# A pair's third key chunk and second half of its queries behind its second query group, the output weights and the half projection one group later

## The chip, the cores and the metric

The kernel runs on one core of a Trainium2 chip. The metric is the device time of one execution in microseconds (us). An execution was also taken by the hardware profiler, which gives each instruction's start and length on the core's engines: TensorE (PE for its matmuls, PEld for its weight loads), VectorE (DVE), ScalarE (ACT), GpSimd (POOL) and SyncE (SP), which here only issues transfers.

## The reference

One layer of a trunk over 1024 frames and 16 meta tokens in front, 1024 channels wide, all in float32. What the change touches is the attention group (8 heads of 64) and the output projection behind it:

```python
u = rms_norm(h, norm_mix_w[l])
proj = u @ w_in[l]
fq, fk, fv, ff, hq, hf, hi, hg = jnp.split(proj, split_at, axis=-1)
...
s = jnp.einsum('bqhd,bkhd->bhqk', q_i, k) * scale
s = s + (c_i[..., :, None] - cT[:, :, None, :])      # c: running sum of the log forget gates
s = jnp.where(key_pos[None, :] <= q_pos[:, None], s, MASK_VALUE)
p = jax.nn.softmax(s, axis=-1)
o = jnp.einsum('bhqk,bkhd->bqhd', p, v)
...
mixed = jnp.concatenate([fox_out, hgrn_out], axis=-1) @ w_out[l]
h = h + mixed
```

`hgrn_out` is a second group, a gated linear recurrence, whose four blocks of 128 channels are finished before the attention starts. After this come a norm, a SwiGLU feed-forward part and a final norm.

## The kernel before, in words

Each float32 operand of a large product is split into a rounded part ("hi") and the rest ("lo"), and a product is three matmuls: hi by hi, hi by lo, lo by hi (`mm3`, lines 166 to 169). ScalarE writes "hi" (a cast), VectorE subtracts to get "lo".

The normed input, transposed and split, stays in on-chip memory as `u` (the pool `uT`). The heads go in four pairs, p = 0 to 3. For a pair, `fox_proj` loads its key and query weights (128 columns each) and makes the keys in three chunks of 348, 346 and 346 frames (`keys(0)` to `keys(2)`) and the queries in two halves of 512 (`queries(0)`, `queries(1)`). Each is 24 matmuls into one "dense" accumulator bank, of which there are three, and is then copied out by ScalarE and VectorE (lines 522, 523 and 530, 531).

`fox_compute` then takes the pair's queries in four groups of 256, g = 0 to 3. A group takes for each of its two heads two tiles of 128 queries: scores (lines 569 and 570, tile `g`, two banks), minimum with the bias on VectorE (line 575), exponential on ScalarE (line 580), transposes (lines 588 and 600), copies split in two parts (lines 604 and 605), and the product with the values (line 610). Before it, GpSimd makes a copy of the queries with the two halves swapped (`QB`, lines 555 and 556) and masks (`dm`, line 563). Because the attention is causal, group 0 needs only the first key chunk, group 1 the second too, and groups 2 and 3 all three. Groups 0 and 1 use the first half of the queries, groups 2 and 3 the second.

`fox_proj` makes `keys(0)` and `queries(0)` at once and hands the remaining three back as `rest`, which `fox_compute` calls after group 0. The next pair's `fox_proj` follows group 3 in the code. The key and query weights of a pair lie in two buffers that the next pair's weights take when they are free; their "lo" part is made by GpSimd (line 136).

The last pair calls `after_group(g)` behind each group. After group 0 it gives up the memory of `u`, opens in its place the pools for the output projection, and loads the output weights of the recurrence's blocks (`WO1`, four tiles of 128 x 1024, through two staging buffers, lines 678 to 684). After group 1 it computes `out_half`: the recurrence's part of the output projection for the first two tiles of frames (48 matmuls), and loads the other four weight tiles (`WO2`). Behind the attention follow `out_proj` for the eight tiles of frames, the norm and the feed-forward part.

The order of the code is not the order on the engines. The library with which the program is built orders each engine's instructions by its own estimate of when their operands are ready, and takes the order of the code between those that are. So projections of a pair stand between the matmuls of the group that precedes them in the code, and a transfer is issued when a buffer comes free. On the chip each engine runs its list in order.

Of the kernel before, what the change touches and what calls it, by code (L numbers as in the profile page):

```python
# [44 lines left out]
def f32(ap):  # L45
    return ap.bitcast(F32)
# [3 lines left out]
def hybrid_trunk(  # L50
# [71 lines left out]
    def bank(tag, bufs=None):  # L122
        return (psg if tag in ("g", "o") else ps).tile([P, 512], F32, name=tag, tag=tag, **({"bufs": bufs} if bufs else {}))
# [30 lines left out]
    def load_m(c0, wsrc, engine=None):  # L154
        st = w1.tile([P, KT, P], F32, name="w_st", tag="w_st")
        sync.dma_start(out=st, in_=wsrc.rearrange("(k p) c -> p k c", p=P)[:, :, c0:c0 + P])
        hi = w1.tile([P, KT, P], F32R, name="w_hi", tag="w_hi")
        lo = w1.tile([P, KT, P], F32R, name="w_lo", tag="w_lo")
        split(hi, lo, st, engine)
        return hi, lo  # L160
# [10 lines left out]
    def form1(u, w, c0, n):  # L171
        o = dense()
        hi, lo = w
        for k in range(KT):
            mm3(o[:, :n], hi[:, k, :], lo[:, k, :], u[0][:, k, c0:c0 + n], u[1][:, k, c0:c0 + n], k == 0, k == KT - 1)
        return o[:, :n]
# [205 lines left out]
    def keys(out, R, lev):  # L382
        R6 = R.rearrange("p (k r t) -> p r k t", k=2, r=2)
        Z = (out if lev == 1 else out[:, :256])
        for r in range(2):
            if lev == 1:
                Zr = Z.rearrange("p (k r t) -> p r k t", k=2, r=2)[:, r]
                src = R6[:, r]
            else:
                Zr = Z.rearrange("p (k t) -> p k t", k=2)  # L390
                src = R6[:, r].rearrange("p k (a s b) -> p k a s b", s=2, b=lev)[:, :, :, 0, :]
            if r:
                Zr = Zr[:, :, ::-1]
            if lev > 1:
                Zr = Zr.rearrange("p k (a s b) -> p k a s b", s=2, b=lev)[:, :, :, 0, :]
            act.activation(Zr, src, AF.Exp, scale=-1.0)
# [115 lines left out]
    def fox_proj(p, fxk):  # L512
        KS = [fxk.tile([P, L], F32R, name=f"KS{j}", tag=f"KS{j}") for j in range(2)]
        QA = [fxk.tile([P, SEQ], F32R, name=f"QA{j}", tag=f"QA{j}") for j in range(2)]
        wk, wq = (load_m(c + p * P, w_in[0], pool if p else None) for c in (C_FK, C_FQ))
        lanes = [(0, slice(0, 64), slice(64, 128)), (1, slice(64, 128), slice(0, 64))]

        def keys(i):
            c0, n = FULL[i]
            o = form1(u, wk, c0, n)  # L520
            for j, a, b in lanes:
                act.copy(KS[j][a, c0:c0 + n], o[a])
                vec.tensor_sub(KS[j][b, c0:c0 + n], o[a], f32(KS[j][a, c0:c0 + n]))

        def queries(i):
            c0, n = REAL[i]
            o = form1(u, wq, c0, n)
            q = slice(c0 - META, c0 - META + n)
            for j, a, b in lanes:
                act.activation(QA[j][a, q], o[a], AF.Copy, scale=-0.125)  # L530
                vec.scalar_tensor_tensor(QA[j][b, q], o[a], -0.125, f32(QA[j][a, q]), ALU.mult, ALU.subtract)

        keys(0)
        queries(0)
        return KS, QA, lambda: (keys(1), keys(2), queries(1))

    def fox_head_load(p, j, pool_):
        h = 2 * p + j
        vt = pool_.tile([P, NT + 1, P], F32R, name=f"v{j}", tag=f"v{j}", bufs=1)
        sync.dma_start(out=f32(vt[:, :NT, :]), in_=v_dram[:NT, :, h, :].rearrange("t p c -> p t c"))  # L540
        pool.memset(f32(vt[:, NT, :]), 0.0)
        for r0 in (0, 32):
            sync.dma_start(out=f32(vt[r0:r0 + META, NT, :]), in_=v_dram[NT, :META, h, :])
        nl = pool_.tile([P, L], F32, name=f"nl{j}", tag=f"nl{j}", bufs=1 if p == 0 else 2)
        sync.dma_start(out=nl, in_=nl_dram[h, :].partition_broadcast(P))
        tg = small.tile([P, 4], F32, name=f"tg{j}", tag=f"tg{j}", bufs=2)
        vec.tensor_scalar(tg[:, 0:4], nl[:, META + 255::256], -1.0, None, ALU.mult)
        return vt, nl, tg
# [78 lines left out]
    def fox_compute(p, KS, QA, rest, heads=None, extra=None):  # L627
        heads = heads or [fox_head_load(p, j, fx) for j in range(2)]
        for g in range(4):
            mixp = fx.tile([P, 256], F32, name="mixp", tag="mixp")  # L630
            rr = small.tile([P, 2, 2], F32, name="rr", tag="rr")
            for j in range(2):
                fox_group(p, j, g, KS[j], QA[j], *heads[j], rr, mixp)
            rw = fx.tile([P, 2, P], F32, name="rw", tag="rw", bufs=1)
            pool.tensor_copy(rw.rearrange("p i (j d) -> p (i j) d", d=HD), rr.rearrange("p i j -> p (i j)").unsqueeze(2).to_broadcast([P, 4, HD]))
            rb = bank("tr")
            for ii in range(2):
                pe.transpose(rb[:, ii * P:(ii + 1) * P], rw[:, ii, :], ident)
            vec.tensor_mul(mixp, mixp, rb[:, :256])
            sync.dma_start(out=mix_dram[p, :, 256 * g:256 * (g + 1)], in_=mixp)  # L640
            if g == 0:
                rest()
            if extra:
                extra(g)
    a = hgrn_proj(0)
# [13 lines left out]
    fx0 = fx0_pool.__enter__()  # L659
    heads0 = [fox_head_load(0, j, fx0) for j in range(2)]  # L660
    b = fox_proj(0, fxk0)
    hg_pool.__exit__(None, None, None)
    fx_pool, fxk1_pool = right("fx", 2), right("fxk1")
# [4 lines left out]
    for s in range(3):  # L668
        fox_compute(s, *b, heads0 if s == 0 else None)
        if s == 0:  # L670
            fx0_pool.__exit__(None, None, None)
        b = fox_proj(s + 1, (fxk0, fxk1)[(s + 1) % 2])
# [3 lines left out]
    def load_wo(ks):  # L676
        for k in ks:
            st = w1.tile([P, D], F32, name="w_st", tag="w_st")
            sync.dma_start(out=st, in_=w_out[0, k * P:(k + 1) * P, :])
            hi = wo.tile([P, D], F32R, name=f"woh{k}")  # L680
            lo = wo.tile([P, D], F32R, name=f"wol{k}")
            act.copy(hi, st)
            for hs in (slice(0, 512), slice(512, 1024)):
                vec.tensor_sub(lo[:, hs], st[:, hs], f32(hi[:, hs]))
            wos[k] = (hi, lo)
# [4 lines left out]
    def out_half(ts):  # L690
        mt, mh, ml = (op.tile([P, KT, P], d, name=n_, tag=n_, bufs=1) for n_, d in (("mt", F32), ("mh", F32R), ("ml", F32R)))
        for i, t in enumerate(ts):
            a = slice(4 * i, 4 * i + 4)
            sync.dma_start(out=mt[:, a, :], in_=mix_dram[4:8, :, t * P:(t + 1) * P].rearrange("k p c -> p k c"))
            split(mh[:, a, :], ml[:, a, :], mt[:, a, :])
        for i, t in enumerate(ts):
            halves[t] = op.tile([P, D], F32, name="h2", tag="h2")
            for hs in (slice(0, 512), slice(512, 1024)):
                o = dense()
                for k in range(4):  # L700
                    j = 4 * i + k
                    mm3(o, mh[:, j, :], ml[:, j, :], wos[4 + k][0][:, hs], wos[4 + k][1][:, hs], k == 0, k == 3)
                act.copy(halves[t][:, hs], o)

    def after_group(g):
        nonlocal op, wo
        if g == 0:
            uT_pool.__exit__(None, None, None)
            op, wo = op_pool.__enter__(), wo_pool.__enter__()
            load_wo(WO1)  # L710
        if g == 1:
            out_half(ORDER[:2])
            load_wo(WO2)

    fox_compute(3, *b, None, after_group)
    fxk1_pool.__exit__(None, None, None)
    fx_pool.__exit__(None, None, None)
# [477 lines left out]
```

## Time and profile before

| | |
|---|---|
| time of three runs | median 1305.54 us (1304.8 to 1307.61) |
| profiled execution | 1305.52 us, span 1303.8 us |
| TensorE busy | 1270.7 us, 97% of the span |
| VectorE busy | 909.3 us, 70% |
| ScalarE busy | 621.2 us, 48% |
| GpSimd busy | 125.9 us, 10% |
| mean granted TensorE clock | 0.995 |

The span runs from the first instruction's start to the last one's end. A matmul's row shows about 0.39 us for 512 columns although the next starts 0.23 us later, because matmuls overlap; the distance of starts is what one costs. The time in brackets behind a row is the engine's idle time before it, and behind the arrow stands what ended it. A row of a transfer on SyncE is its issue; it lands microseconds later.

### The profile page before, as it was taken

To read this page: it belongs to the slowest core of one execution; us is meant where nothing else is said; L and a number is where in the kernel's file an instruction comes from. 1 tells how busy PE (TensorE), PEld (TensorE's weight loads), DVE (VectorE), ACT (ScalarE), POOL (GpSimd) and SP (SyncE) were. 2 spreads that over 40 slices of the span, in tenths; PEclk is the share of its full clock that TensorE was granted. 3 is DMA by queue.
4 is the path that set the end of the run, shared out by engine and by line. 5 is a ranking of instruction groups with operands and counts; after the bars stand their busy time and mean duration, and the time that the engine had idled before them with its cause. 6 is when DMAs were issued, how large, how long until landed. Compare 5 with 4: busy or idle time off the path is not lost.

```text
span 1303.8 us, 18528 instructions
## 1 busy us (share of the span) xinstructions
PE 1270.7 (97%) x6553; PEld 1065.4 (82%) x6553; DVE 909.3 (70%) x1889; ACT 621.2 (48%) x1334; POOL 125.9 (10%) x257
## 2 busy tenths in 40 slices
PE   7999999999999999899999999999999999999997
PEld 6888898988888888688868888888888888888886
DVE  6448657574687877796798766666666654697777
ACT  6347656464666665664453333233323323433364
POOL 1131101010334342210000000000000000000000
PEclk8999999999999999999999999999999999999999
DMA  7232212123321211633314323333332336954442
GB/s 253 73 98 58 74 44 73 58 58 118 92 79 45 69 52 47 187 100 119 125 49 138 125 83 115 121 111 103 118 121 74 113 121 248 317 188 151 121 169 82
DMA packets 135197, 146.38 MB, mean 112 GB/s; under 512 B 6984, under 2 KB 95368, under 8 KB 135104
## 3 DMA queue, kind: packets, MB, share of 16 engines
q1 hardware_dynamic: 135104, 145.19, 34.6%
q8 instruction: 52, 0.85, 0.3%
q14 instruction: 41, 0.34, 0.1%
HBM read 105.98 MB, written 39.19 MB: 111 GB/s over the span
## 4 chain that ended last, share of the span: by engine, by line
PE 80%; DVE 8%; ACT 5%; DMA 3%; issue 2%; POOL 2%; SPq 0%; POOLq 0%; DVEq 0%; ACTq 0%
PE pb L167 10%; PE pb L169 10%; PE pb L168 10%; PE dense L169 8%; PE dense L167 8%; PE dense L168 8%; PE g L169 4%; PE g L167 4%; PE g L168 4%; PE o L610 2%; PE tr L600 2%; PE g L569 1%; PE g L570 1%; PE g L446 1%; DMA w_st<-in_w_in_dram 1%
## 5 line engine op out<-in xcount | busy, mean ns | idle before, releaser
L167 PE MATMUL dense<-u_hi,w_hi 128*128 128x512 f32 (+2 forms) x384 | 141.7, 369 | 0.0
L169 PE MATMUL dense<-u_hi,w_lo 128*128 128x512 f32 (+2 forms) x384 | 141.3, 368 | 0.0
L168 PE MATMUL dense<-u_lo,w_hi 128*128 128x512 f32 (+2 forms) x384 | 140.9, 367 | 0.0
L168 PE MATMUL pb<-T_lo,bh 128*128 128x512 f32 x352 | 137.2, 390 | 0.2
L169 PE MATMUL pb<-T_hi,bl 128*128 128x512 f32 x352 | 137.1, 390 | 0.1
L167 PE MATMUL pb<-T_hi,bh 128*128 128x512 f32 x352 | 136.9, 390 | 0.2 <-ACT bh L135 0.2
L135 ACT CAST bh<-sS 128x512 fp32r<-128x512 f32 x88 | 54.3, 621 | 144.3 <-PE pb L168 70.3
L135 ACT CAST h_hi<-h_st 128x1024 fp32r<-128x1024 f32 (+1 forms) x43 | 41.8, 971 | 83.7 <-PE o L168 38.2
L168 PEld LDWEIGHTS pb<-T_lo,bh 128*128 128x128 f32 x352 | 66.1, 188 | 15.0 <-DVE T_lo L136 1.1
L169 PEld LDWEIGHTS dense<-u_hi,w_lo 128*128 128x128 f32 x384 | 72.9, 190 | 6.2
L167 PEld LDWEIGHTS pb<-T_hi,bh 128*128 128x128 f32 x352 | 66.1, 188 | 14.6 <-ACT bh L135 0.6
L167 PEld LDWEIGHTS dense<-u_hi,w_hi 128*128 128x128 f32 x384 | 72.6, 189 | 6.5
L168 PEld LDWEIGHTS dense<-u_lo,w_hi 128*128 128x128 f32 x384 | 72.6, 189 | 6.4
L169 PEld LDWEIGHTS pb<-T_hi,bl 128*128 128x128 f32 x352 | 66.1, 188 | 14.2 <-DVE bl L136 0.4
L167 PE MATMUL pb<-w_hi,h_hi 128*128 128x512 f32 x198 | 77.3, 391 | 0.0
L169 PE MATMUL pb<-w_hi,h_lo 128*128 128x512 f32 x198 | 77.2, 390 | 0.0
L168 PE MATMUL pb<-w_lo,h_hi 128*128 128x512 f32 x198 | 77.2, 390 | 0.0
L136 DVE TENSOR_TENSOR w_lo<-w_st,w_hi 128x1024 fp32r<-128x1024 f32 (+1 forms) x41 | 49.6, 1210 | 35.4 <-ACT w_hi L135 35.4
L136 DVE TENSOR_TENSOR h_lo<-h_st,h_hi 128x1024 fp32r<-128x1024 f32 (+1 forms) x43 | 48.3, 1124 | 30.2 <-ACT h_hi L135 29.9
L167 PE MATMUL g<-B_hi,w_hi 128*128 128x512 f32 x168 | 66.6, 396 | 0.9 <-ACT p L865 0.9
L169 PE MATMUL g<-B_hi,w_lo 128*128 128x512 f32 x168 | 66.5, 396 | 0.0
L168 PE MATMUL g<-B_lo,w_hi 128*128 128x512 f32 x168 | 66.3, 395 | 0.0
(861 smaller groups left out, 3328.5 us busy)
## 6 DMA issues: line engine op xcount, KB each, us to landing
w_st<-in_w_in_dram SPq DMA_DIRECT2D x24, 512.0 KB, 4.2
w_st<-in_w_ffn_gate_dram SPq DMA_DIRECT2D x22, 512.0 KB, 3.8
w_st<-in_w_ffn_up_dram SPq DMA_DIRECT2D x22, 512.0 KB, 3.9
B<-in_w_ffn_down_dram SPq DMA_DIRECT2D x20, 512.0 KB, 6.3
h_st<-S SPq DMA_DIRECT2D x20, 512.0 KB, 3.8
h_st<-A SPq DMA_DIRECT2D x15, 512.0 KB, 4.4
A<-g SPq DMA_DIRECT2D x22, 256.0 KB, 2.0
S<-u SPq DMA_DIRECT2D x22, 256.0 KB, 3.0
```

Source lines behind the costliest of these rows:

```text
L135: later(act.copy(hi, src))
L136: return later((engine or vec).tensor_sub(lo, src, f32(hi)))
L167: pe.matmul(o, lhsT=ah, rhs=bh, start=first, stop=False, skip_group_check=skip)
L168: pe.matmul(o, lhsT=ah, rhs=bl, start=False, stop=False, skip_group_check=skip)
L169: pe.matmul(o, lhsT=al, rhs=bh, start=False, stop=last, skip_group_check=skip)
L446: m = pe.matmul(gb[:, k * P:(k + 1) * P], lhsT=X[:, k * P:(k + 1) * P], rhs=X[:, 256 + k * P:256 + (k + 1) * P], start=True, stop=True)
L569: pe.matmul(sc[:, :w], lhsT=QA[:, P * i:P * (i + 1)], rhs=KS[:, c0:c0 + w], start=True, stop=False)
L570: pe.matmul(sc[:, :w], lhsT=QB[:, P * ii:P * (ii + 1)], rhs=KS[:, c0:c0 + w], start=False, stop=True)
L600: pe.transpose(pt[:, o + ii * P:o + (ii + 1) * P], Ss[ii][:, c:c + P], ident)
L610: m = pe.matmul(ob[:, q0:256], lhsT=vt[:, blk, :], rhs=r[:, q0:256], start=blk == NT, stop=blk == 2 * g + 1 and i == 3)
```

## The change

`fox_proj` hands back two functions in place of one: the first makes the second key chunk, the second makes the third key chunk and the second half of the queries. `fox_compute` calls the first after group 0 and the second after group 1. In the last pair, giving up the memory of `u` and loading `WO1` move from behind group 0 to behind group 1, and `out_half` and `WO2` from behind group 1 to behind group 2.

```diff
@@ fox_proj
         keys(0)
         queries(0)
-        return KS, QA, lambda: (keys(1), keys(2), queries(1))
+        return KS, QA, (lambda: keys(1), lambda: (keys(2), queries(1)))
@@ fox_compute
             sync.dma_start(out=mix_dram[p, :, 256 * g:256 * (g + 1)], in_=mixp)
-            if g == 0:
-                rest()
+            if g < 2:
+                rest[g]()
             if extra:
                 extra(g)
@@ after_group
         nonlocal op, wo
-        if g == 0:
+        if g == 1:
             uT_pool.__exit__(None, None, None)
             op, wo = op_pool.__enter__(), wo_pool.__enter__()
             load_wo(WO1)
-        if g == 1:
+        if g == 2:
             out_half(ORDER[:2])
             load_wo(WO2)
```

## Prediction

> **What bounds the kernel now.** I read the page first (engine shares), then a table of busy time by stage over the attention part, then the order of time on TensorE, ScalarE, GpSimd and SyncE in the one stage that stood out. A row of the table gives start:end, length, and busy microseconds of PE, PEld, DVE, ACT and POOL, then the granted clock, the DMA share and GB/s.
>
> ```profile
> span 1303.8 us, 18528 instructions
> PE 1270.7 (97%) x6553; PEld 1065.4 (82%) x6553; DVE 909.3 (70%) x1889; ACT 621.2 (48%) x1334; POOL 125.9 (10%) x257
> 397.00:424.00 27.00, 26.45 (x168) 22.25 (x168) 20.96 (x71) 19.10 (x48) 14.25 (x28) 1.00 0.19 50
> 424.00:447.00 23.00, 22.93 (x156) 19.62 (x155) 21.12 (x73) 15.70 (x31) 6.71 (x18) 1.00 0.19 58
> 447.00:470.00 23.00, 22.84 (x147) 20.30 (x145) 13.71 (x49) 13.41 (x33) 8.98 (x16) 1.00 0.28 83
> 470.00:503.00 33.00, 32.42 (x217) 28.14 (x215) 29.43 (x105) 22.69 (x50) 12.20 (x30) 1.00 0.09 25
> 503.00:524.00 21.00, 20.45 (x130) 18.03 (x129) 11.98 (x36) 9.20 (x26) 5.27 (x16) 1.00 0.22 65
> 524.00:535.00 11.00, 6.50 (x29) 4.34 (x29) 8.22 (x23) 6.12 (x10) 4.64 (x8) 1.00 0.76 237
> 548.00:564.00 16.00, 14.99 (x82) 11.46 (x80) 15.24 (x46) 10.81 (x24) 4.98 (x11) 1.00 0.44 127
> 564.00:585.00 21.00, 20.66 (x136) 17.79 (x137) 19.13 (x59) 13.95 (x32) 1.01 (x3) 1.00 0.26 84
> ```
>
> TensorE is the bound: 97% of the span. The change adds and removes no arithmetic, so it can win only TensorE's idle time in the stages it touches, and can lose only by making more. Pairs 1 and 2 (397 to 503 us) hold 0.55 + 0.07 + 0.16 + 0.58 = 1.4 us of it. The last pair (503 to 585) holds far more: in 524 to 535 TensorE stands still for 11.00 - 6.50 = 4.5 us, with 0.55 before, and 1.01 and 0.34 in its groups 2 and 3. This is the order of time there, TensorE first, the idle time in brackets:
>
> ```profile
> 516.77 0.37 PE L167 MATMUL dense<-u_hi,w_hi 128*128 128x346 f32 x1
> 518.73 0.40 PE L167 MATMUL dense<-u_hi,w_hi 128*128 128x512 f32 x1
> 524.06 0.39 PE L169 MATMUL dense<-u_hi,w_lo 128*128 128x512 f32 x1
> 524.29 0.34 PE L569 MATMUL g<-KS,QA 128*128 128x400 f32 x1
> 524.65 0.29 PE L569 MATMUL g<-KS,QA 128*128 128x264 f32 x1
> 526.56 0.36 PE L569 MATMUL g<-KS,QA 128*128 128x264 f32 x1 [1.50 <-DVE mx L575]
> 528.38 0.28 PE L588 MATMUL tr<-ident,S__6394 128*16 128x128 f32 x1 [1.34 <-ACT S__6394 L580]
> 528.89 0.50 PE L167 MATMUL dense<-woh,mh 128*128 128x512 f32 x1
> 534.80 0.50 PE L167 MATMUL dense<-woh,mh 128*128 128x512 f32 x1 [1.54 <-ACT woh L682]
> 547.50 0.39 PE L169 MATMUL dense<-woh,ml 128*128 128x512 f32 x1
> 547.73 0.31 PE L569 MATMUL g<-KS,QA 128*128 128x328 f32 x1
> 515.22 0.52 DVE L523 TENSOR_TENSOR KS<-dense,KS 64x346 fp32r<-64x346 f32 x1
> 524.49 0.59 ACT L530 ACTIVATE QA<-dense 64x512 fp32r<-64x512 f32 x1 [4.10 <-PE dense L169]
> 524.98 1.98 ACT L682 CAST woh<-w_st 128x1024 fp32r<-128x1024 f32 x2
> 533.70 1.04 ACT L682 CAST woh<-w_st 128x1024 fp32r<-128x1024 f32 x1 [4.34 <-DMA w_st<-in_w_out_dram]
> 543.90 1.04 ACT L682 CAST woh<-w_st 128x1024 fp32r<-128x1024 f32 x1
> 551.34 1.05 ACT L682 CAST woh<-w_st 128x1024 fp32r<-128x1024 f32 x1 [1.37 <-DMA w_st<-in_w_out_dram]
> ```
>
> Group 1's keys are complete at 515.74 (515.22 + 0.52), yet its first score starts only at 524.29: the third key chunk and the second half of the queries (346 and 512 columns), which group 1 does not need, stand ahead of it. Then group 1 runs with nothing beside it. TensorE waits 1.50 us for VectorE's minimum, 1.34 us for the exponential, and 1.54 us for an output-weight cast that waited 4.34 us for its transfer: 4.38 us, nearly all of the hole.
>
> **The change, part by part.** *Third key chunk and second query half behind group 1.* In the last pair what is left of them from 516.6 on is 7.7 us of matmuls (516.6 to 524.3; rows below). The last 24, of 512 columns, go from 518.73 to 524.29, 0.232 us each. Group 1 itself, by tile:
>
> ```profile
> 516.60:524.30 7.70, 7.53 (x36) 6.34 (x36) 1.03 (x2) 0.89 (x2) 1.00 0.06 19
> 524.30:547.70 23.40, 13.96 (x49) 8.29 (x48) 1.38 (x2) 2.82 (x5) 1.00 0.68 214
> 547.70:564.00 16.30, 8.51 (x29) 5.00 (x28) 1.36 (x2) 0.59 (x1) 1.00 0.43 125
> ```
>
> These are the instructions on the projection accumulators alone: 48 weight loads, so 48 matmuls, in group 1's stretch, which are the half projection's: 48 x 0.232 = 11.1 us. Group 1's own TensorE time is then 23.4 - 4.5 - 11.1 = 7.8 us. With the change it starts at about 516.6 beside the 7.7 us of projections and is done at 516.6 + 7.8 + 7.7 = 532.1, its waits filled: **-4.4 us** (1.50 + 1.34 + 1.54). If the projections still run as a block ahead of it, 0.
>
> *Group 2 now stands right behind its projections.* It needs the second query half, so its chain starts only when that half is copied out. From the last projection matmul, 24 x 0.232 us after the first, to the first out-projection matmul that could fill was 528.89 - 524.06 = 4.8 us; the two score chunks for which there are banks fill 2 x 0.36 = 0.7 us of it (524.29 to 524.65 for a chunk), so up to 4.1 us stand open, and the cast's 1.54 us can come again: 5.6 us. The lower end is 0: the planner may drain the query half between group 1's waits, so that group 1's tail covers the copies. Both rows are as near as they get; since the planner ranks the query half behind all of group 1, some of it must be last, but 7.7 us cannot all be, with 4.4 us of holes to fill in group 1. That leaves (7.7 - 4.4) / 7.7 = 43% of the block contiguous, and I take the same share of the wait, 0.43 x 5.6 = **+2.4 us**.
>
> *Output weights and half projection one group later.* Eight transfers, eight casts on ScalarE, sixteen subtractions on VectorE, four splits and 48 matmuls move; none is added. What starts the ladder is the end of the last projection, whose operand's room the weights take: 524.3 before, about 532.1 after, so 7.8 us later by time although one group later by order. Cost on the path: the 5.6 us above and the rival below. The queues it is moved past:
>
> ```profile
> 536.13 11.74 SPq L679 DMA_DIRECT2D w_st<-in_w_out_dram  x4
> 548.40 0.33 SPq L640 DMA_DIRECT2D mix_dram<-mixp  x1
> 461.75 1.05 ACT L135 CAST w_hi<-w_st 128x1024 fp32r<-128x1024 f32 x1 [1.32 <-PE dense L168]
> 462.88 2.40 POOL L136 TENSOR_TENSOR w_lo<-w_st,w_hi 128x1024 fp32r<-128x1024 f32 x1 [7.99 <-ACT w_hi L135]
> ```
>
> On SyncE the last four weight loads wait for free buffers over 11.7 us, and group 1's store of its mix is queued behind them; after, it is group 2's store. Its reader comes only after the pair, so it costs 0; with that cover gone, it would cost about the delay that the queue has, under 12 us, on one tile.
>
> *The other pairs.* The next pair's weights are cast when the key matmuls free a buffer (461.75, behind a projection matmul), so these 1.05 us and GpSimd's 2.40 us move one group later too, ahead of group 2's query copies; in pairs 0 to 2 the next pair's first projections fill behind them. They cost 0 there, and 2.40 us a pair on the path if that cover were gone. Their gain is bounded by the idle time above, 1.4 us in pairs 1 and 2; I take 0, between -1.4 and +1.4, since idle time is already as low ahead of group 1 (447 to 470: 0.16) as within the groups.
>
> **The sum.** -4.4 + 2.4 + 0 = -2.0 us against the profiled execution, 1305.52 us (span 1303.8, 1.7 around it), which stands within 0.02 us of the median of the runs, 1305.54. Forecast: **1303.5 us**, 0.15% less, inside the 0.2% (2.6 us) that a measurement of this kernel can tell from no change. Its own range is 1302.0 to 1305.0.
>
> **Rivals.** *The hole closes for good* (faster): the query half is drained inside group 1, group 2's chain overlaps group 1's tail, and pairs 1 and 2 give some of their 1.4 us. 1305.5 - 4.4 - 0.6 = 1300.5 us. For it: VectorE and ScalarE are at 11.98 and 9.20 of 21 us in 503 to 524 and have room. Against: group 2 needs both copies of the queries before any score.
>
> *The hole moves whole* (the change does not do what it says): all 5.6 us stand in front of group 2, less 4.4 saved: 1306.7. For it: the same ladder of two buffers, the same cast ahead of the same kind of exponential. Pair 0 and 1 may see no move at all, since the planner already ran projections ahead of their group (TensorE idles 0.55 us in 27 in pair 1).
>
> *The weights come too late for group 3* (slower): the half projection is used up in front of group 3, and the output projection that fills group 3 has no weights yet. The last cast came 551.34 - 524.3 = 27.0 us after the ladder's start, so at 559.1 after; the second of those four casts came at +19.6 (543.90), at 551.7 after. Group 2 and the half projection need 16.3 - 1.0 - 28 x 0.232 = 8.8 and 11.1 us from 532.1, so with the 2.4 us group 3 starts at about 554.4. It decides when group 3 starts before 551.7: then it lacks up to 559.1 - 554.4 = 4.7 us of filler. Price: group 2's 2.4 us and these 4.7 less 4.4 saved, 1308.2 us, and more if VectorE, at 15.24 of 16 us in 548 to 564, also has the weights' subtractions there.
>
> *GpSimd held up by VectorE.* The weight subtractions now stand beside group 2's query copies and masks.
>
> ```profile
> 506.34 0.29 POOL L563 TENSOR_SCALAR_AFFINE_SELECT dm<-nl 128x128 f32<-128x128 f32 x1
> 526.48 0.68 POOL L563 TENSOR_SCALAR_AFFINE_SELECT dm<-nl 128x128 f32<-128x128 f32 x1 [14.94 <-DVE mx L575]
> 509.00 0.39 POOL L555 CAST QB<-QA 64x256 fp32r<-64x256 f32 x1 [2.37 <-PE g L570]
> 527.23 0.73 POOL L555 CAST QB<-QA 64x256 fp32r<-64x256 f32 x1
> ```
>
> The mask took 0.29 us alone and 0.68 beside them, a copy 0.39 and 0.73. With one mask and two copies ahead of group 2's second score matmul that is 0.39 + 2 x 0.34 = 1.1 us more on its chain: 1304.6 us. The Trainium skill, SBUF — State Buffer, section "Who interferes with whom", says that a VectorE instruction with two SBUF inputs and a GpSimd instruction that reads SBUF exclude each other for the whole instruction, so it speaks against moving these subtractions to where GpSimd's copies gate the scores. By that rule the loss is as large as a full subtraction each time; the trace agrees in kind, with 0.34 to 0.39 us each.
>
> **How the numbers follow.** Chances: forecast 0.38 (of it 0.10 under 1302.9), hole closes 0.27, hole moves whole 0.12 (0.01 of it above 1308.1), too late for group 3 0.19, GpSimd 0.04. Faster by over 0.2%: 0.10 + 0.27 = 0.37. Slower: 0.01 + 0.19 = 0.20. Within: 0.43. The range goes from the closing case's lower end, 1305.5 - 4.4 - 1.4 less some of the 1.35 us that groups 2 and 3 of the last pair stand idle, 1299.0, to the slower case's price, 1308.5; beyond the ends lies some 0.1 each side.
>
> **What the profile after would show.** Right: the first 400-column score of the last pair at about 517, no TensorE wait over 1 us in group 1, and between the last projection matmul and the first output-projection matmul a hole of 2 to 3 us in front of group 2. Wrong: a hole of 4 us or more there (moved whole), none (closed), or a new wait for an output-weight cast within group 3 (slower). Idle time in pairs 0 to 2 that moves by over 1.5 us would show that my zero for them failed; so would a planner's order that differs outside the attention.

## The result, and the profile after

The changed kernel took 1309.03 us (median of its timing, 1307.09 to 1312.04), the kernel before 1305.64 in the same one: a ratio of 1.0027, 95% interval [1.0019, 1.0035]. It is 0.27% slower, above the forecast of 1303.5 and above the range's upper end of 1308.5. One run of each kernel in that timing was far slower than its others (2577.79 us after, 1359.93 before) and is in neither the ratio nor the range; it was the changed kernel's that was profiled, so the profile shown here is of a second timing (e1). That one gave 1308.27 against 1304.52, 1.0035 [1.0022, 1.0049]; its profiled execution took 1307.18 us, span 1305.5.

The columns of the rows by stage are those of the prediction's table: start:end, length, busy time of PE, PEld, DVE, ACT and POOL, granted clock, DMA share, GB/s. Since both kernels pass a stage at other times, I cut at the same events: the first exponential of pair 0, of pair 1, of pair 2 and of the last pair, the last one's end, and the first feed-forward matmul. Before:

```profile
355.10:397.80 42.70, 40.84 (x274) 35.65 (x274) 36.49 (x138) 27.77 (x66) 17.46 (x47) 1.00 0.28 91
397.80:447.60 49.80, 49.18 (x321) 41.59 (x320) 41.98 (x144) 34.62 (x80) 20.81 (x44) 1.00 0.19 54
447.60:503.10 55.50, 54.76 (x357) 48.09 (x356) 42.76 (x147) 35.56 (x80) 20.73 (x44) 1.00 0.17 49
503.10:576.60 73.50, 67.25 (x394) 55.31 (x391) 57.73 (x166) 44.79 (x96) 17.66 (x40) 1.00 0.42 130
sum 316.40, PE 304.53 PEld 254.98 DVE 248.10 ACT 189.52 POOL 77.09; mean PE 60.91 PEld 51.00 DVE 49.62 ACT 37.90 POOL 15.42
```

After:

```profile
353.70:395.60 41.90, 40.80 (x275) 35.62 (x274) 36.50 (x138) 27.75 (x66) 17.48 (x47) 1.00 0.29 91
395.60:449.30 53.70, 51.62 (x348) 44.99 (x346) 45.20 (x151) 37.11 (x85) 21.71 (x46) 1.00 0.20 61
449.30:506.70 57.40, 55.65 (x346) 48.60 (x346) 41.14 (x145) 33.73 (x77) 21.76 (x47) 0.97 0.12 38
506.70:574.20 67.50, 60.80 (x353) 49.71 (x351) 53.94 (x155) 42.23 (x89) 16.25 (x35) 0.97 0.42 126
sum 319.90, PE 305.88 PEld 257.54 DVE 248.36 ACT 189.53 POOL 77.59; mean PE 61.18 PEld 51.51 DVE 49.67 ACT 37.91 POOL 15.52
```

The sums, which hold the five stretches up to the first feed-forward matmul, differ by 3.5 us, as much as the timings do. Length less PE busy is TensorE's idle time: 11.87 before, 14.02 after, 2.15 us more. The other 1.35 us are in PE's busy time although the work is the same, and the granted clock, 1.00 in every row of before, is 0.97 in two of after.

By stage the idle time is: pairs 1 and 2 together 0.62 + 0.74 = 1.36 before and 2.08 + 1.75 = 3.83 after; the last pair 6.25 and 6.70; pair 0 1.86 and 1.10. So the pairs that the forecast took at zero lost 2.47 us, and the pair that was to win 2.0 won nothing. TensorE's waits for GpSimd's swapped queries (`QB`) from 395 to 505 us, pairs 1 and 2 (what it waited for, us in total, times, the longest), say where. Before, then after:

```profile
PE g L570 <- POOL QB L556: 0.4, 1, 0.4
```

```profile
PE g L570 <- POOL QB L555: 2.6, 2, 1.5
```

The 0.4 us of before stand at 504.69, in the last pair's first group; pairs 1 and 2 had no such wait. The two of after, one a pair, are about as long together as the 2.47 us that these pairs lost. GpSimd's order of time after, in pair 2:

```profile
474.17 2.38 POOL L136 TENSOR_TENSOR w_lo<-w_st,w_hi 128x1024 fp32r<-128x1024 f32 x1 [4.84 <-ACT w_hi L135]
476.61 0.39 POOL L556 CAST QB<-QA 64x256 fp32r<-64x256 f32 x1
477.06 0.74 POOL L555 CAST QB<-QA 64x256 fp32r<-64x256 f32 x2
```

The next pair's weight subtraction, 2.38 us, stands directly ahead of the swapped queries of group 2, and TensorE waits for them:

```profile
475.48 0.57 PE L569 MATMUL g<-KS,QA 128*128 128x328 f32 x2
477.51 0.57 PE L570 MATMUL g<-KS,QB 128*128 128x328 f32 x2 [1.47 <-POOL QB L555]
477.92 0.42 PE L169 MATMUL dense<-u_hi,w_lo 128*128 128x348 f32 x1
...
479.58 0.49 PE L169 MATMUL dense<-u_hi,w_lo 128*128 128x348 f32 x1
479.88 0.49 PE L167 MATMUL dense<-u_hi,w_hi 128*128 128x348 f32 x1
```

The next pair's projections were there to fill, but in TensorE's list they come behind the waiting matmul. They also run slowly: 479.88 - 479.58 = 0.30 us apart, where matmuls of the same 348 columns were 0.16 us apart before the hole (473.82 to 473.98).

The subtraction stood ahead of these copies in the kernel before too, with one mask of 0.29 us between. GpSimd, then TensorE, before:

```profile
468.36 2.40 POOL L136 TENSOR_TENSOR w_lo<-w_st,w_hi 128x1024 fp32r<-128x1024 f32 x1 [3.08 <-ACT w_hi L135]
471.07 0.39 POOL L556 CAST QB<-QA 64x256 fp32r<-64x256 f32 x1
471.52 0.40 POOL L555 CAST QB<-QA 64x256 fp32r<-64x256 f32 x1
472.87 0.40 PE L569 MATMUL g<-KS,QA 128*128 128x328 f32 x1
473.11 0.31 PE L570 MATMUL g<-KS,QB 128*128 128x328 f32 x1
```

There it cost nothing. Until group 2's first score, at 472.87, TensorE had group 1 and the next pair's projections to work on, and group 1's last product of values came only at 479.78. After, that product stands at 469.87, and group 2's first score at 475.48 finds its swapped queries still in GpSimd's queue. What the change took away is group 1's work as cover.

The last pair after, TensorE from the end of the projections to the half projection:

```profile
532.02 0.39 PE L169 MATMUL dense<-u_hi,w_lo 128*128 128x512 f32 x1
533.81 0.57 PE L569 MATMUL g<-KS,QA 128*128 128x328 f32 x2 [1.40 <-DVE QA L531]
536.24 0.79 PE L167 MATMUL dense<-woh,mh 128*128 128x512 f32 x1 [1.40 <-ACT mh L135]
```

Group 1's first score now starts at 514.98, and no wait over 0.3 us stands in group 1. But the last matmuls of the query half still end ahead of group 2's first score, and two waits of 1.40 us stand there.

### The profile page after: what moved, and what is told of

Its sections match the earlier page's. It is cut to its first block, busy times and chain, and to the rows that moved or that the text cites. A ratio compares the mean times of both kernels' runs of the same rounds, so it can differ in the third digit from the quotient of the medians.

```text
span 2576.1 us, 18549 instructions
## 1 busy us (share of the span) xinstructions
PE 2561.6 (99%) x6553; PEld 1802.6 (70%) x6553; DVE 917.5 (36%) x1889; ACT 629.9 (24%) x1334; POOL 120.4 (5%) x257
## 4 chain that ended last, share of the span: by engine, by line
PE 99%; ACT 0%; DVE 0%; issue 0%; POOL 0%; POOLq 0%
PE pb L168 12%; PE pb L167 12%; PE pb L169 12%; PE dense L167 11%; PE dense L168 11%; PE dense L169 11%; PE g L167 5%; PE g L169 5%; PE g L168 5%; PE o L610 3%; PE tr L600 3%; PE g L446 1%; PE g L569 1%; PE g L570 1%; PE tr L149 1%; PE o L168 1%
## 5 line engine op out<-in xcount | busy, mean ns | idle before, releaser
L167 PE MATMUL dense<-u_hi,w_hi 128*128 128x512 f32 (+2 forms) x384 | 245.7, 640 | 0.0
L169 PE MATMUL dense<-u_hi,w_lo 128*128 128x512 f32 (+2 forms) x384 | 244.9, 638 | 0.0
L168 PE MATMUL dense<-u_lo,w_hi 128*128 128x512 f32 (+2 forms) x384 | 244.0, 635 | 0.0
L169 PE MATMUL pb<-T_hi,bl 128*128 128x512 f32 x352 | 237.4, 675 | 0.0
L168 PE MATMUL pb<-T_lo,bh 128*128 128x512 f32 x352 | 237.1, 674 | 0.0
L167 PE MATMUL pb<-T_hi,bh 128*128 128x512 f32 x352 | 236.4, 672 | 0.0
L167 PE MATMUL pb<-w_hi,h_hi 128*128 128x512 f32 x198 | 133.6, 675 | 0.0
L169 PE MATMUL pb<-w_hi,h_lo 128*128 128x512 f32 x198 | 133.5, 674 | 0.0
L168 PE MATMUL pb<-w_lo,h_hi 128*128 128x512 f32 x198 | 133.4, 674 | 0.0
L167 PE MATMUL dense<-woh,mh 128*128 128x512 f32 x128 | 87.8, 689 | 1.1 <-ACT mh L135 1.1
```

Of the source, the lines that this page charges most:

```text
L167: pe.matmul(o, lhsT=ah, rhs=bh, start=first, stop=False, skip_group_check=skip)
L168: pe.matmul(o, lhsT=ah, rhs=bl, start=False, stop=False, skip_group_check=skip)
L169: pe.matmul(o, lhsT=al, rhs=bh, start=False, stop=last, skip_group_check=skip)
```

## The experiments

The diffs are against the changed kernel, that of e7 and e8 apart, which is against e2 and the kernel before.

**e1_after: the changed kernel again, beside its parts.**

> The changed kernel as it stands, for a profile beside its time. Theory A (the last pair loses: the hole of 4.4 us that stood in its group 1 comes back larger in front of its group 2, or in group 3 for want of output weights): about 1309 us, TensorE idle between the start of the last pair and 640 us at least 3 us over the 6.8 us of before, pairs 1 and 2 within 1 us of their 1.4 us. Theory B (pairs 0 to 2 lose: their groups stall on the later projections): the extra idle time stands before 503 us. Theory C (the clock: a longer hole lowers the granted clock): idle time about as before, and a mean granted clock 0.002 to 0.003 under that of before.

1308.27 us, 1.0035 [1.0022, 1.0049]; the rows above are from it. Most of the extra idle time stands in pairs 1 and 2, as theory B has it; the last pair does not have the 3 us more of theory A. The mean granted clock of the runs is 0.9930 against 0.9951 before, as theory C has it, but the idle time is not as before.

**e2_pairs012: only pairs 0 to 2 changed.** The last pair calls both functions after group 0, and `after_group` is as before.

```diff
-            if g < 2:
-                rest[g]()
+            if g < 2 and p < 3:
+                rest[g]()
+            if g == 0 and p == 3:
+                rest[0]()
+                rest[1]()
```

> Pairs 0 to 2 changed, the last pair as before. Theory A: 1305.5 us, within 1 us of before. Theory B: 1308 to 1309 us, with the extra idle time before 503 us. Theory C: as before, since the last pair's hole is the old one.

1307.03 us, 1.0024 [1.0015, 1.0033]; the wait for QB is 2.6 us, as in the whole change. The time lies between theory A's and theory B's.

**e3_pair3: only the last pair changed**, with its output weights (the mirror of e2's edit).

> Only the last pair changed: its third key chunk and second query half behind its group 1, output weights and half projection one group later; pairs 0 to 2 as before. Theory A: 1308 to 1309 us. Theory B: 1303 to 1305 us. Theory C: 1308 to 1309 us with a lower mean granted clock.

1306.39 us, 1.0010 [1.0001, 1.0019], again between the theories: both parts lose.

**e4_weights: only the output weights one group later**, all projections in their old places (`g == 0` to `g == 1` and `g == 1` to `g == 2` in `after_group`, nothing else).

> All projections where they were before; only the output weights and the half projection go one group later in the last pair. If the late weights are what the last pair loses by, 1308 us or more: group 1 keeps a hole of 4 us or so (nothing fills it, not even the half projection) and groups 2 and 3 lack filler. If the chain from the late query half to group 2 is what it loses by, about 1305 to 1306 us, since that chain is as before here. Theory B: 1305.5 us.

1302.87 us, 0.9992 [0.9983, 1.0000], under every time expected. So the change has three parts: pairs 0 to 2 cost 0.24%, the last pair's projections 0.10 + 0.08 = 0.18%, and the output weights give 0.08% back, which is at the edge of what this timing can tell from nothing; the sum, 0.34%, agrees with the 0.27 to 0.35% that was measured. TensorE's longer waits in the last pair (505 to 590 us) of e3, then of e2, whose last pair has the code of before, then of e4:

```profile
PE g L569 <- DVE mx L575: 1.9, 2, 1.5
PE g L569 <- DVE QA L531: 1.4, 1, 1.4
PE dense L167 <- ACT mh L135: 1.4, 1, 1.4
PE tr L588 <- ACT S__6640 L580: 0.8, 1, 0.8
PE dense L167 <- ACT woh L685: 0.5, 1, 0.5
```

```profile
PE g L569 <- DVE mx L575: 1.7, 2, 1.5
PE tr L588 <- ACT S__6394 L580: 1.3, 1, 1.3
PE tr L600 <- DVE mz L591: 0.6, 1, 0.6
PE o L610 <- DVE mz L591: 0.4, 1, 0.4
PE tr L588 <- ACT S__6634 L580: 0.4, 1, 0.4
```

```profile
PE g L569 <- DVE mx L575: 2.5, 4, 1.5
PE tr L588 <- ACT S__6359 L580: 0.9, 1, 0.9
PE g L570 <- POOL QB L556: 0.4, 1, 0.4
```

With the projections in their old place group 1 keeps its two waits, 1.5 and 1.3 us in e2 and 1.5 and 0.9 in e4. With them behind group 1 these go, and those for the query copies, the half projection's cast and the weights come: with the small ones 6.5 us in all in e3, against 4.4 in e2 and 4.3 in e4.

The 1.54 us for the output-weight cast, which the profile of before has, is in none of e2, e4 and e8 (below) and is 0.5 us in e7, although e2, e7 and e8 load the output weights as before. So its absence in e4 is not shown to come from the moved weights, and no profile here shows where their 0.08% would come from. What sets the profile of before apart is its clock: it is granted 1.00 throughout its last pair, and these four have a stretch of half clock there.

**e5_qfirst and e6_keys_only: other orders behind group 1.** e5 makes the query half before the third key chunk; e6 leaves the queries behind group 0 and moves the key chunk alone. Both apply to all pairs.

```diff
-        return KS, QA, (lambda: keys(1), lambda: (keys(2), queries(1)))
+        return KS, QA, (lambda: keys(1), lambda: (queries(1), keys(2)))      # e5
+        return KS, QA, (lambda: (keys(1), queries(1)), lambda: keys(2))      # e6
```

> As changed, but behind group 1 the second query half comes ahead of the third key chunk. Theory D (what costs is the chain from the last query projection over its copies and GpSimd's swapped copy to group 2's first scores, with nothing on TensorE beside it): the 3.9 us of the key chunk now cover that chain in the last pair, so its 1.40 us wait for the copied queries goes and the half-clock stretch behind it shrinks: 1 to 3 us faster than the changed kernel, 1305 to 1307 us against 1304.5 of before. Theory R (any projection placed later costs, whatever follows it): as the changed kernel, 1308 us.

1309.25 us, 1.0030 [1.0018, 1.0041]: a miss for theory D.

> Only the third key chunk stands behind group 1; both query halves are made before it; the weights of the last pair as changed. Theory D: the query copies are long done when group 2 starts, so the waits for them are gone in all pairs: 1303 to 1305 us, like the kernel with the weights alone one group later (1302.9). Theory R: about half of the loss, 1306 us.

1308.38 us, 1.0025 [1.0013, 1.0036]: a miss too. The wait did go where the theory saw it: TensorE waits 0.4 us for QB in 395 to 505 us in e5, and less than the view lists in e6; in the last pair the 1.40 us for the query copies is gone from both. But with the new order a loss stands at the start of pair 0. Busy time in 300 to 360 us, before, then e5, then e6:

```profile
300.00:360.00 60.00, 57.71 (x381) 51.19 (x379) 37.01 (x105) 32.85 (x111) 13.13 (x29) 1.00 0.34 101
```

```profile
300.00:360.00 60.00, 55.09 (x362) 49.06 (x361) 35.01 (x97) 32.74 (x109) 11.59 (x25) 1.00 0.31 97
```

```profile
300.00:360.00 60.00, 56.26 (x374) 50.35 (x372) 34.30 (x93) 31.88 (x107) 10.24 (x20) 1.00 0.31 94
```

TensorE is idle 2.3 us there before, 4.9 in e5 and 3.7 in e6: pair 0 starts beside the last part of the recurrence (before, its first score stands at 341.05 us and matmuls of the recurrence go on to 349), and the library mixes the two another way. An edit to the order of all pairs thus tests more than its place, and neither run tells the theories apart.

**e7_dve and e8_before_dve: GpSimd's subtraction.** The low part of the query weights of pairs 1 to 3 is made by VectorE, in e2 and, as the control, in the kernel before.

```diff
-        wk, wq = (load_m(c + p * P, w_in[0], pool if p else None) for c in (C_FK, C_FQ))
+        wk, wq = (load_m(c + p * P, w_in[0], pool if p and c == C_FK else None) for c in (C_FK, C_FQ))
```

> Pairs 0 to 2 changed and the last pair as before, but the low part of the query weights is subtracted by VectorE (1.2 us) in place of GpSimd (2.4 us). Theory D: the waits of 1.46 and 1.14 us for GpSimd's query copies in front of group 2 of pairs 1 and 2 go, and with them the half-clock stretch of 3.4 us in pair 2 (some 1.5 us): 1304 to 1305 us against 1307 with GpSimd. Theory R: 1307 us as with GpSimd.

1304.49 us, 0.9994 [0.9985, 1.0003].

> The kernel before with the same subtraction on VectorE, as the measure for the run above. Theory D: within 1 us of before, since GpSimd's subtraction had no one waiting for it there beyond 0.4 us. Theory R says nothing on it; if it gains 2 us or more, the run above shows the engine and not the order.

1304.68 us, 0.9994 [0.9984, 1.0004]. Both hit: with it pairs 0 to 2 lose nothing (1.0024 becomes 0.9994), and the kernel before with the same edit is not told apart from the one without. VectorE's subtraction, 1.2 us, thus costs nothing that shows. In e7 GpSimd's order of time has no subtraction in front of the copies:

```profile
467.59 0.41 POOL L635 COPY rw<-rr 128x256 f32<-128x256 f32 x1
475.17 0.77 POOL L556 CAST QB<-QA 64x256 fp32r<-64x256 f32 x1 [7.18 <-ACT QA L530]
476.46 0.40 POOL L555 CAST QB<-QA 64x256 fp32r<-64x256 f32 x1 [0.52 <-DVE QA L531]
```

GpSimd now waits 7.18 us for the queries, not they for it, and the view of waits of e7 has none for QB.

**e9_after_dve: the whole change with that edit.**

> The whole change, with the low part of the query weights of pairs 1 to 3 subtracted by VectorE instead of GpSimd. Theory G (in pairs 1 and 2 the loss is GpSimd's 2.4 us subtraction standing ahead of group 2's swapped queries): the waits of TensorE for QB in 395 to 505 us fall from 2.6 us to under 0.8, and the time to that of the last pair's change alone, 1306 to 1307 us against 1304.5 to 1305.5 before. Rival H (moving the projections costs whichever engine subtracts, because the last pair and the planner's order make up for it): 1308 or more. Rival S (only pairs 0 to 2 ever lost): at or under the time before.

1305.99 us, 1.0010 [1.0001, 1.0019]: the last pair's ratio alone (e3), and 2 us under rival H. No wait for QB is left in pairs 1 and 2. Theory G holds, and the two losses are separate.

**e10_weights_dve: the two edits that did not lose, together**, e4 with the subtraction on VectorE.

> All projections in their old places; only the output weights and the half projection one group later, and the query weights' low part subtracted by VectorE. If the two gains add (about 1.6 us for the output weights, 0.5 to 0.7 us for VectorE in the kernel before): 1302 to 1303 us, faster than both kernels by 0.15 to 0.25%. If the earlier gain of the output weights was only the order of that one run: 1304 to 1305. If VectorE's added 1.1 us a pair meets the output weights' sixteen subtractions in the last pair: over 1305.

1303.71 us, 0.9992 [0.9983, 1.0000], no better than e4: the gains do not add. Beside e9 it shows the last pair's projections a second time, at the same 0.18%. With e4 it is the best version seen, 0.08% under the kernel before, less than can safely be told from nothing.

**e11_fill: useless work in two holes of the changed kernel.**

```diff
+                if g == 2 and p == 2 and j == 0 and ii == 0 and c0 == 0:
+                    for _ in range(10):
+                        pe.matmul(sc[:, :w], lhsT=nil, rhs=KS[:, c0:c0 + w], start=False, stop=False)
                 pe.matmul(sc[:, :w], lhsT=QB[:, P * ii:P * (ii + 1)], rhs=KS[:, c0:c0 + w], start=False, stop=True)
@@ out_half, first accumulator
+                    for f in range(6):
+                        pe.matmul(o, lhsT=nil, rhs=wos[4][0][:, hs], start=f == 0, stop=False)
```

> The whole change with useless work in two of its holes: ten matmuls of 328 columns with a weight of zeros between the two halves of the first score of pair 2's group 2, and six of 512 columns ahead of the half projection's first one; together about 2.9 us of TensorE work that changes no value. Theory C (a hole costs twice, the second time because the granted clock is halved for 3.41 us behind it): no stretch of half clock at about 478 or 536 us, mean granted clock up from 0.993 to 0.9945 or more, and the time equal to the changed kernel's or up to 2 us under it although work is added. Rival N (the clock stretches are no matter of the holes): the stretches stay, the time stays or rises by up to 2.9 us.

1308.90 us, 1.0033 [1.0020, 1.0046]. The fillers took the place of the wait for QB in pair 2 and of most of that for `mh` (0.2 us are left), and the profile has no stretch of half clock between the start and the end of the program; the mean granted clock over the timed runs was 0.9952 (e1: 0.9930; the kernel before beside each: 0.9947 and 0.9951). Yet the time did not fall. So in this profile the halved clock went with the holes, against N, and 2.9 us of work fit into them at no cost that shows, but that the halved clock costs time is not shown: the library also rearranged pair 2's third group around the filler, and this may have cost what the clock gave.

**e12_last_q: of the last pair's projections only the third key chunk behind group 1**, the query half behind group 0; pairs 0 to 2 as before, output weights one group later.

```diff
+            if g == 0:
+                rest[0]()
+                if p < 3:
+                    rest[1]()
+                rest[2]()
+            if g == 1 and p == 3:
+                rest[1]()
```

> Only the last pair and the output weights changed, and of the last pair's projections only the third key chunk stands behind group 1; the second half of the queries stays behind group 0. Theory Q (the last pair loses because group 2 waits for the query projection's copies and then for the half projection's cast, 1.40 us each, and group 3 for a minimum): these waits of TensorE go, the sum of its waits in the last pair falls from 6.5 us to 4.3 to 5.0, and the time comes to within 1 us of the kernel with the output weights alone moved, 1303 to 1304.5 us. Rival V (any part of the projections that leaves the place behind group 0 opens group 1's hole again without closing another, since the output weights' room then comes free as late as with the whole move): waits of 6 us or more, 1306 us or over.

1304.80 us, 0.9999 [0.9990, 1.0008], 0.3 us above Q's band and well under V's. Its waits in the last pair:

```profile
PE tr L588 <- ACT S__6539 L580: 1.5, 1, 1.5
PE o L610 <- DVE mixp L622: 1.5, 1, 1.5
PE g L569 <- DVE mx L575: 1.1, 3, 0.7
```

With two of 0.2 us they come to 4.5, with none for the query copies or `mh`. The 0.11% between e3 and this point at the query half as the larger part of the last pair's loss. That is likely and not shown: the two were timed apart and their intervals overlap, and so do those of this run and of e4, which would show what the key chunk costs.

## Why the prediction was wrong

Two steps failed: the zero for pairs 0 to 2, and the net of -2.0 us for the last pair.

*Pairs 0 to 2 at zero.* The text saw GpSimd's 2.40 us "ahead of group 2's query copies", named the price "2.40 us a pair on the path if that cover were gone", and chose zero because the next pair's first projections would fill. They could not: on TensorE the score matmul stands ahead of them in the list, and a list waits as a whole. The text also read the subtraction as moving ahead of the copies. In pair 2 it stood there already in the kernel before; the cover was group 1's own work, and the change took that away. Measured: 1.1 and 1.5 us of wait for QB, 2.47 us of idle time in two pairs, half of the named price, and 0.24% of the time (e2); e2, e7 and e9 show that it is this subtraction. My own mark, idle time in pairs 0 to 2 that moves by over 1.5 us, was passed (3.22 to 4.93). The argument that idle time is low ahead of group 1 bounded the gain and said nothing of a loss at group 2. Whether it is the 2.4 us in the queue alone, or also the order of TensorE that the library chose because of it, is not separated.

*-4.4 us in group 1: right in kind, too large.* Its waits went, and its first score came even earlier than the 517 us forecast. But 1.54 of the 4.4 us, the wait for the output-weight cast, belong to the one execution that the sum was taken from: e2, e7 and e8 have 0, 0.5 and 0 us of it with the last pair's code of before, so there group 1 had 2.8 us to give.

*+2.4 us in front of group 2: near, but not all.* The two waits of 1.40 us there, 2.8 us, lie in the 2 to 3 us that the text forecast. So, against e2, the hole moved whole: 2.8 us went from group 1 and 2.8 came in front of group 2. What the sum put at nothing is the idle time behind that: in e1 waits for the weights (0.6 us), for an exponential (1.1) and, in group 3, for a minimum (1.7). Besides the 2.8 us, e3 has 3.7 us of waits and e2 1.6. The rows of the last pair, first exponential to the last one's end, of e2, e3 and e4:

```profile
507.20:577.80 70.60, 65.95 (x379) 54.17 (x377) 56.03 (x161) 44.43 (x96) 16.32 (x35) 0.98 0.43 135
502.70:573.90 71.20, 64.66 (x368) 52.80 (x365) 55.48 (x160) 43.09 (x90) 18.03 (x40) 0.95 0.38 119
503.90:572.70 68.80, 64.50 (x369) 53.12 (x367) 54.96 (x160) 43.20 (x90) 17.62 (x40) 0.95 0.40 124
```

TensorE is idle 4.65 us in e2 and 4.30 in e4, and 6.54 in e3, as in the whole change (6.70). Only beside the profile of before, with its 6.25 us at full clock, does the last pair look unchanged. By the timings it costs 0.10% (e3), some 1.3 us where the forecast had -2.0: near the 1.2 us that the "hole moves whole" rival gave, with part of it later than that rival says. Why the waits behind group 2 grew is not shown. The output weights and the projections were priced together; by e3 and e4 the projections alone cost 0.18%.

*Weights too late for group 3: wrong in kind.* In the changed kernel the last output-weight cast started as late as 560.49 us, but group 3's wait, 1.69 us, is for VectorE's minimum; the one wait for a weight cast, 0.6 us, stands earlier, at 543.94.

*GpSimd held up by VectorE: right in kind, not in the place.* Two query copies of the last pair took 0.92 and 0.82 us beside the output weights' subtractions where they take 0.39, and a mask 1.21 beside another subtraction of VectorE; no wait for QB is listed in the last pair.

*The clock was left out.* The prediction quoted a granted clock of 1.00 in every row and treated it as given. The changed kernel's profile has two stretches of half clock in the attention, and 1.35 us of its 3.5 us are longer busy time; e11 leaves open how much of that is loss. The clock also changes the holes themselves: the last pair of before has 6.25 us of idle time at clock 1.00, and the same code in e2 4.65 at 0.98.

## What to carry to other kernels

Where work is moved behind a group, look at every in-order engine that the next group's first operands pass, not only at the engine that is the bound, and ask what covered that path until now. A 2.4 us instruction on an engine 10% busy stood ahead of two 0.4 us copies at no cost while another group's work ran beside it, and became a wait on TensorE when that work was done too early. Filler helps only if it stands ahead of the waiting instruction in the list. Take the size of a hole from more than one execution: here a wait of 1.54 us in the profile that the forecast used was absent from two of three others with the same code. Time each part of an edit by itself: two parts lost 0.24 and 0.18%, a third may have gained 0.08%, and the sum hid all three.

## What the runs showed of the hardware

A hole in TensorE's work well under 3 us can halve its clock for the next 3.41 us. Whether it does depends on how the hole falls on a grid of 3.41 us on which the clock changes. Busy time on that grid in the changed kernel, pair 2:

```profile
474.59:478.00 3.41, 1.88 (x11) 1.33 (x10) 1.41 (x3) 0.71 (x2) 3.23 (x5) 1.00 0.11 38
478.00:481.41 3.41, 3.41 (x14) 3.41 (x13) 1.62 (x7) 0.00 (x0) 0.55 (x2) 0.50 0.30 115
```

And the hole of the kernel before in its last pair, larger but spread over two windows of its grid:

```profile
523.55:526.97 3.42, 1.93 (x10) 1.42 (x9) 2.05 (x7) 2.47 (x3) 0.49 (x1) 1.00 0.37 106
526.97:530.38 3.41, 1.94 (x9) 1.20 (x8) 3.32 (x8) 2.35 (x5) 1.68 (x3) 1.00 0.85 190
530.38:533.79 3.41, 2.88 (x13) 1.89 (x12) 2.63 (x12) 0.09 (x1) 2.06 (x4) 1.00 0.90 338
```

Over the thirteen profiles here, the start and the end of the program left out, all twelve full-clock windows with at most 1.55 us busy of 3.41 were followed by a window at half clock, none with 1.92 or more was, and from 1.58 to 1.89 both are found. So here about half a window of work held the clock. In e8 the same hole as before's fell into one window with 1.30 us busy, and the next had half clock: whether such a hole halves the clock varies from run to run. The clock goes with the time: in the timing beside e1, the nine runs of the kernel before at a mean clock of 0.994 took 1305.2 us on average, the four at 0.997 1302.8, though that alone does not say which causes which. The Trainium skill, TensorE: Matmul & The Clock Gate, section "Part 1: The HAM clock gate", has a free-running window of 3413 ns and half rate after a window that was idle; the length agrees with the 3.41 us here, but the windows above were not idle, only about half so. Its section "Why this matters for your kernels" advises against gaps over about 3 us; by the windows above about 1.5 us idle within one window can be enough, and the measurement decides.
